# Spare columns between the on-chip tiles of a hybrid decoder layer: operands at 0, 32, 64 and 96 modulo 128 bytes

## The chip, the cores and the metric

The kernel runs on one core of a Trainium2 chip. The metric is the device time of one execution in microseconds. A core has five engines that run side by side: TensorE (PE, with its weight loads shown apart as PEld), VectorE (DVE), ScalarE (ACT), GpSimd (POOL) and SyncE (SP), which issues most of the DMAs. On-chip memory (SBUF) has 128 partitions; a tile lies at one byte offset, the same on every partition. PE sums its products in PSUM.

## The reference

One layer (DEPTH 1) for 512 tokens of width 1024, all in float32:

```python
mod = (cond @ w_ada[l] + b_ada[l])[:, None, :]
sh1, sc1, g1, sh2, sc2, g2 = jnp.split(mod, 6, axis=-1)
h = _rms(x, norm1_w[l]) * (1 + sc1) + sh1
x = x + g1 * _hybrid_mixer(h, w_in[l], ...)
h = _rms(x, norm2_w[l]) * (1 + sc2) + sh2
x = x + g2 * (jnp.square(jax.nn.relu(h @ w_ff1[l])) @ w_ff2[l])
```

`_hybrid_mixer` multiplies h by w_in (1024 x 11,280 columns) and splits the result into the parts of three mixers: a state-space scan (SSD), an attention in three dilated groups, and a pooling over four windows. Each mixer has an output projection and a sigmoid gate; their gated sum goes through w_out.

## The kernel before

**Products in three matmuls.** Every large product runs with operands split into a high and a low part of type float32r (`split`, L310, for activations; `wsplit`, L267, for weights), and `mm3` (L284) issues three matmuls for one block: high weights with low x, high weights with high x, low weights with high x. A matmul has a stationary operand (`lhsT`, 128 columns, loaded before it) and a moving one (`rhs`, 512 columns, 256 where tokens are halved).

`gemm_feat` (L289) has the weights stationary and the activations moving; `gemm_tok` (L301) has the activations stationary (128 tokens of the 512, either next to each other or, with `mod`, every fourth one) and the weights moving. The weights stream in by `wstream` (L274): a DMA of two row blocks, a high part on ScalarE (L270), a low part on VectorE (L271), in three buffers each.

**Names.** hh and hl are the high and low parts of the first normed input, 8 tiles each; gh and gl, in the same places, those of the second. wh and wl are the streamed weights; wsh and wsl those of the first two chunks, Q and K, loaded apart; wrh and wrl weights that are kept (`resident`, L1054). ah and al are the parts of the squared ReLU; yn, pool, mx, o and pd those of the SSD output, the pooling, the gated sum, the attention output and the pooled differences. In the profile a matmul's operands stand as moving, stationary: `psacc<-gl,wh` moves gl over weights wh.

**Order.** The Q and K products of the first chunk (up to some 65 us), and the stretch from the second half of the output projection to the first MLP chunk, are in an order written out by hand; the rest is laid out by the scheduler, with `wstream`'s loads and splits ahead of other work. Pieces of attention, SSD and modulation are handed out between row blocks of weights.

**Where tiles lie.** Pools follow one another in SBUF, and inside a pool each tile follows the one before. cpool holds `cst` (the constants, L159, 328 columns) and then hh0..hh7 and hl0..hl7, 2048 bytes each. sm holds small tiles; raws and wsp the raw and split weights; gp the 59 blocks of 128 x 512 that `Slots` (L116) hands out, the one first that has been free for longest. All other activations and kept weights live in these blocks. In the built program hh and hl start at 32 modulo 128 bytes, all of them; wh, wl and every block of gp start at 96.

Of the kernel before, what the change touches and what calls it, by code (L numbers as in the profile page):

```python
# [28 lines left out]

# [1 line left out]
def _alibi_slopes(n):  # L31
# [53 lines left out]

# columns of the vector table: 128 values each
VCOLS, _at = {}, 0
# [5 lines left out]

# chunks of 512 columns of w_in
Z, XS, BCC, Q, K, VV, U, GS, GA, GP = 0, 2, 4, 5, 8, 11, 14, 16, 18, 20
# [3 lines left out]
def kernel(ctx: ExitStack, tc: tile.TileContext, a: dict, out: bass.AP, dbg=None):  # L99
# [16 lines left out]
    class Slots:  # L116
        """places of [128, 512] float32: the one that has been free for longest goes first"""

        def __init__(self, pool, prefix, n):
            self.pool, self.prefix = pool, prefix  # L120
            self.idle, self.used = list(range(n)), {}

        def take(self, name, dt):
            i = self.idle.pop(0)
            t = self.pool.tile([P, T], dt, tag=f"{self.prefix}{i}", name=uid(name), bufs=1)
            self.used[id(t)] = (i, t)
            return t
# [3 lines left out]

    sb, banks = Slots(gp, "b", NBLK), Slots(pp, "p", 8)

# [22 lines left out]

# [1 line left out]
    ncut = COFF["al0"][0]  # L158
    cst = cpool.tile([P, ncut], F32, name="cst")  # L159

# [21 lines left out]

    # 1/sqrt(sum/n + eps) of a small tile of sums
    def rsqrt_small(ss, n, name):
# [9 lines left out]
    def token_rsqrt(sums, n, name):  # L194
        """1/sqrt(sum over the partitions of sums / n + eps) on every partition, in PSUM"""
        nb = sums.shape[1] // P
        sp = psm(name)
        for b in range(nb):
            mm(sp[:, b : b + 1], lhsT=sums[:, b * P : (b + 1) * P], rhs=ones[:, 0:1], start=True, stop=True)
        ss = small([P, 4], name, 2)[:, :nb]  # L200
        V.tensor_copy(ss, sp[:, :nb])
        free(sp)
        return spread(rsqrt_small(ss, n, name + str(nb)), nb, name)

    def spread(r, nb, name):
        """columns of tokens to rows, the same on every partition, in PSUM"""
        rp = psm(name)
        for b in range(nb):
            dg = small([P, P], "diag", 2)
            V.tensor_scalar(dg, ident, r[:, b : b + 1], None, ALU.mult)  # L210
            mm(rp[:, b * P : (b + 1) * P], lhsT=ones, rhs=dg, start=True, stop=True)
        return rp
# [11 lines left out]

# [1 line left out]
    def ada_load(part, k):  # L226
# [20 lines left out]

    # work beside the large products: handed out one piece per two row blocks of weights
    background = [ada_later(part, k) for part in (2, 3, 4, 5) for k in range(8)]
# [15 lines left out]

# [1 line left out]
    def wsplit(raw, shape):  # L267
# [21 lines left out]
    def gemm_feat(w, nk, ch, ah, al, k0=0):  # L289
        """4 blocks [128 columns of w, 512 tokens]"""  # L290
        ps = [acc() for _ in range(4)]
        for k, wh, wl in wstream(w, nk, ch, k0):
            for j in range(4):
                cs = slice(j * P, (j + 1) * P)
                mm3(ps[j], wh[:, cs], wl[:, cs], ah[k], al[k], k == 0, k == nk - 1)
        return ps
# [4 lines left out]
    def gemm_tok(w, nk, ch, ah, al, mod, ahead=None):  # L301
        """4 blocks [128 tokens, 512 columns of w]; tokens 128 b + p, or 4 p + b with mod"""
        ps = [acc() for _ in range(4)]
# [12 lines left out]
    def evac(ps, name, func=AF.Copy):  # L316
        """out of PSUM, ahead of other work"""
        with tc.high_priority(offset=SOON):
# [10 lines left out]

# [1 line left out]
    E = mybir.EngineType  # L331
    with tc.manual_schedule(engines={E.DVE, E.Activation, E.PE, E.SP}):
# [101 lines left out]
        hh = [cpool.tile([P, T], F32R, name=f"hh{k}", tag=f"hh{k}") for k in range(8)]  # L434
        hl = [cpool.tile([P, T], F32R, name=f"hl{k}", tag=f"hl{k}") for k in range(8)]

# [25 lines left out]
        for k in range(8):  # L462
# [19 lines left out]
            for ch, ps in ((Q, qps), (K, kps)):  # L482
# [3 lines left out]
                free(wh, wl)  # L486
    nc.sync.dma_start(cst[:, P:], a["const"][:, P:ncut])
    free(R1)
# [3 lines left out]

# [1 line left out]
    def take(ps, name):  # L494
        """blocks of q or k out of PSUM, and 1/rms of their heads"""
        xs, ss = evac(ps, name), small([P, 16], "ss" + name, 2)
# [23 lines left out]
    def scores(gi, qs, rq, ks):  # L520
        """pieces of work: transposes of a head, then its scores and exponentials"""
        mx, zs = small([P, 16], f"mx{gi}"), small([P, 16], f"zs{gi}")
# [65 lines left out]
    def exchange(src, mask, sel, name):  # L588
        """[P, 2, (head, i)] -> [P, 2, (head, j)] in the other order of tokens"""
        ps = psm(name)  # L590
# [25 lines left out]
    def joint(stats):  # L616
        """softmax over the three groups: (max, sum) move between the two orders of tokens"""
        (m0, z0), (m1, z1), (m2, z2) = stats
# [20 lines left out]
    def attn_turn(h, probs, fs):  # L639
        """weighted probabilities with keys on partitions"""  # L640
        res = []
# [34 lines left out]

# [1 line left out]
    mixed, mh, ml = [], [], []  # L678
# [25 lines left out]

# [1 line left out]
    v3 = lambda t: t.rearrange("p (c h) -> p c h", h=16)  # L706
    st = {}

    def ssd_steps():
        """step sizes dt [token, (chunk, head)]; p_cum = -a_cum = cumsum(dt exp(a_log)) inside each chunk"""  # L710
        nc.sync.dma_start(hv.rearrange("p a h -> p (a h)"), a["hvec"].broadcast_to([P, 48]))
# [4 lines left out]
        nc.sync.dma_start(wdt, a["w_dt"])  # L716
        # the two parts of the weights side by side
        wd = small([P, 8, 32], "wd", dt=F32R)
# [22 lines left out]
        free(dT, tp)  # L741
        # softplus(x) = max(x, 0) + log1p(e), e = exp(-|x|); log1p(e) = 2 atanh(q), q = e / (2 + e) <= 1/3
        V.tensor_scalar(e, dt, -1.0, None, ALU.mult)
# [27 lines left out]
        yield  # L771
        # rows of p_cum
        tp = psm("pcT")
# [19 lines left out]
    def ssd_states(g, xs, BC):  # L793
        """X = xs dt in token layout, states before each chunk, masked C B^T"""
        BT, CT = BC[g], BC[2 + g]
# [43 lines left out]
    def ssd_heads(g, j, xs, z):  # L839
        """two heads: [128 features, 512 tokens], times silu(z)"""  # L840
        X, prev, cb, CT = st[g]
        pc, npc, prow = st["pc"], st["npc"], st["prow"]
        # p_cum of a head on every partition
        Ms = [blk("M") for _ in range(2)]
# [53 lines left out]

# [1 line left out]
    def pool(half):  # L900
# [36 lines left out]

# [1 line left out]
    yh, yl, dh, dl, ph_, pl_ = [], [], [], [], [], []  # L939
    def pieces(gen):  # L940
        """a generator's steps, as pieces of work"""
        def step():
            next(gen, None)
        return step
# [33 lines left out]
    def do_heads(g, xs, z):  # L978
        # the exponentials of the next two heads stand before the products of these
        gens = [ssd_heads(g, j, xs, z) for j in range(4)]  # L980
# [68 lines left out]

# [1 line left out]
    xT = [blk(f"xr{k}") for k in range(8)]  # L1051
    for k in range(8):
        nc.sync.dma_start(xT[k], a["x"][k])
    def resident(w, ch, k0, n):  # L1054
        """parts of the weights of n row blocks, kept"""
        res = []
# [16 lines left out]
    gh = [cpool.tile([P, T], F32R, name=f"gh{k}", tag=f"hh{k}") for k in range(8)]  # L1073
    gl = [cpool.tile([P, T], F32R, name=f"gl{k}", tag=f"hl{k}") for k in range(8)]
    hw = T // 2
    # the rest of the output projection, the second norm and the first chunk of the MLP, in halves of the tokens:
    # one half's norm runs beside the other half's products
    E = mybir.EngineType
# [100 lines left out]

# [1 line left out]
    def square_relu(ps):  # L1181
# [10 lines left out]
    for half in range(2):  # L1192
# [9 lines left out]
        for ch in range(2):  # L1202
# [5 lines left out]
            else:  # L1208
                # the last rows finish one bank after another, the last bank's tokens in halves
                parts = [(j, full, acc()) for j in range(3)] + [(3, ts, acc()) for ts in halves]  # L1210
# [24 lines left out]
def _laid_out(inputs):  # L1235
    """the inputs in the order in which the kernel reads them"""
    f = {name: np.asarray(inputs[name]) for name in _INS}

    def tiles(w):
        # [K, N] -> [N / 512, K / 256, 128, 2, 512]  # L1240
        k, n = w.shape
        return w.reshape(k // 256, 2, P, n // T, T).transpose(3, 0, 2, 1, 4)
# [32 lines left out]
```

## Time and profile before

| what | value |
|---|---|
| time, median of 3 runs | 1126.01 us (1125.87 to 1126.14) |
| span of the profiled execution | 1123.5 us |
| PE busy | 1116.0 us, 99% of the span, 5414 matmuls |
| weight loads busy | 952.2 us, 85% |
| VectorE busy | 597.9 us, 53% |
| ScalarE busy | 492.2 us, 44% |
| granted TensorE clock | 1.000 |
| DMA | 134.45 MB, mean 120 GB/s |

The profiled execution has no time of its own besides its span; the runs' times hold some 2.5 us more, which lie before the first and after the last instruction of the span. A matmul's record runs from its start to a modelled end and overlaps the next one's, so the time that one matmul takes from the next is read from the starts, or from the count in a stretch.

### The profile page before, as it was taken

To read this page: it belongs to the slowest core of one execution; us is meant where nothing else is said; L and a number is where in the kernel's file an instruction comes from. 1 tells how busy PE (TensorE), PEld (TensorE's weight loads), DVE (VectorE), ACT (ScalarE), POOL (GpSimd) and SP (SyncE) were. 2 spreads that over 40 slices of the span, in tenths; PEclk is the share of its full clock that TensorE was granted. 3 is DMA by queue.
4 is the path that set the end of the run, shared out by engine and by line. 5 is a ranking of instruction groups with operands and counts; after the bars stand their busy time and mean duration, and the time that the engine had idled before them with its cause. 6 is when DMAs were issued, how large, how long until landed. Compare 5 with 4: busy or idle time off the path is not lost.

```text
span 1123.5 us, 14055 instructions
## 1 busy us (share of the span) xinstructions
PE 1116.0 (99%) x5414; PEld 952.2 (85%) x5414; DVE 597.9 (53%) x1210; ACT 492.2 (44%) x937; POOL 0.2 (0%) x4
## 2 busy tenths in 40 slices
PE   8999999999999999999999999999999999999998
PEld 6889998999887888888888888899888888888887
DVE  6973763572667668468833424576354233445241
ACT  5475885543497448425432123353343111344120
POOL 0000000000000000000000000000000000000000
PEclk9999999999999999999999999999999999999999
DMA  9852253333543444322333422360122233322331
GB/s 342 299 183 98 96 164 105 105 104 130 166 135 103 132 142 131 115 83 75 104 113 104 159 94 94 115 204 1 57 93 94 95 101 103 96 95 94 94 131 38
DMA packets 49347, 134.45 MB, mean 120 GB/s; under 512 B 5616, under 2 KB 6384, under 8 KB 49280
## 3 DMA queue, kind: packets, MB, share of 16 engines
q1 hardware_dynamic: 47696, 130.81, 35.6%
q10 hardware_dynamic: 1584, 2.75, 0.8%
q8 instruction: 42, 0.69, 0.2%
q14 instruction: 25, 0.20, 0.1%
HBM read 131.41 MB, written 2.13 MB: 119 GB/s over the span
## 4 chain that ended last, share of the span: by engine, by line
PE 95%; ACT 2%; DVE 2%; DMA 1%; issue 0%; SPq 0%; DVEq 0%; ACTq 0%
PE psacc L285 29%; PE psacc L287 29%; PE psacc L286 29%; PE psS L555 1%; PE psy L867 1%; PE pso L671 1%; PE psyo L875 1%; PE pso L669 1%; DVE conv L786 0%; PE pskT L539 0%; PE psqT L534 0%; PE pspT L652 0%; DVE wa L366 0%; PE psst L827 0%; DMA crow<-in_c_dram 0%; PE pssx L404 0%
## 5 line engine op out<-in xcount | busy, mean ns | idle before, releaser
L271 DVE TENSOR_TENSOR wl<-raw,wh 128x1024 fp32r<-128x1024 f32 x161 | 196.9, 1223 | 348.1 <-ACT wh L270 346.4
L270 ACT CAST wh<-raw 128x1024 fp32r<-128x1024 f32 x161 | 168.9, 1050 | 378.4 <-PE psacc L286 326.2
L285 PE MATMUL psacc<-hl,wh 128*128 128x512 f32 x416 | 168.0, 404 | 0.7 <-ACT prev L830 0.6
L287 PE MATMUL psacc<-hh,wl 128*128 128x512 f32 x416 | 163.2, 392 | 0.0
L286 PE MATMUL psacc<-hh,wh 128*128 128x512 f32 x416 | 162.1, 390 | 0.0
L285 PEld LDWEIGHTS psacc<-hl,wh 128*128 128x128 f32 x416 | 78.3, 188 | 18.0 <-issue 1.2
L287 PEld LDWEIGHTS psacc<-hh,wl 128*128 128x128 f32 x416 | 78.1, 188 | 18.2
L285 PE MATMUL psacc<-wl,hh 128*128 128x512 f32 x224 | 93.4, 419 | 0.0
L286 PEld LDWEIGHTS psacc<-hh,wh 128*128 128x128 f32 x416 | 78.2, 188 | 17.7 <-issue 1.4
L285 PE MATMUL psacc<-al,wh 128*128 128x512 f32 (+1 forms) x242 | 92.1, 381 | 0.0
L286 PE MATMUL psacc<-ah,wh 128*128 128x512 f32 (+1 forms) x242 | 92.1, 381 | 0.0
L287 PE MATMUL psacc<-ah,wl 128*128 128x512 f32 (+1 forms) x242 | 92.1, 380 | 0.0
L286 PE MATMUL psacc<-wh,hh 128*128 128x512 f32 x224 | 90.1, 402 | 0.0
L287 PE MATMUL psacc<-wh,hl 128*128 128x512 f32 x224 | 89.7, 401 | 0.0
L285 PE MATMUL psacc<-gl,wh 128*128 128x512 f32 x224 | 88.3, 394 | 0.0
L287 PE MATMUL psacc<-gh,wl 128*128 128x512 f32 x224 | 87.6, 392 | 0.0
L286 PE MATMUL psacc<-gh,wh 128*128 128x512 f32 x224 | 86.9, 388 | 0.0
L286 PEld LDWEIGHTS psacc<-wh,hh 128*128 128x128 f32 x224 | 65.9, 294 | 1.4
L285 PEld LDWEIGHTS psacc<-wl,hh 128*128 128x128 f32 x224 | 65.5, 293 | 1.7
L287 PEld LDWEIGHTS psacc<-wh,hl 128*128 128x128 f32 x224 | 65.5, 293 | 1.5
L235 DVE SCALAR_TENSOR_TENSOR wa<-wa,crow 128x512 f32<-128x512 f32 x64 | 43.5, 686 | 21.4 <-DMA wa<-in_w_ada_dram 21.3
L285 PEld LDWEIGHTS psacc<-al,wh 128*128 128x128 f32 x242 | 45.5, 188 | 8.9
(342 smaller groups left out, 1914.4 us busy)
## 6 DMA issues: line engine op xcount, KB each, us to landing
raw<-in_w_in_dram SPq DMA_DIRECT2D x80, 512.0 KB, 3.5
raw<-in_w_ff_dram SPq DMA_DIRECT2D x64, 512.0 KB, 3.5
wa<-in_w_ada_dram SPq DMA_DIRECT2D x96, 256.0 KB, 4.6
wst<-in_w_in_dram SPq DMA_DIRECT2D x16, 256.0 KB, 5.4
M<-prow SPq DMA_DIRECT2D x16, 256.0 KB, 3.4
raw<-in_w_ssd_out_dram SPq DMA_DIRECT2D x8, 512.0 KB, 3.5
raw<-in_w_pool_out_dram SPq DMA_DIRECT2D x8, 512.0 KB, 3.4
raw<-in_w_out_dram SPq DMA_DIRECT2D x8, 512.0 KB, 3.4
```

Of the source, the lines that this page charges most:

```text
L235: V.scalar_tensor_tensor(wa[i], wa[i], 1.0, crow[i], ALU.mult, ALU.mult, accum_out=d[:, i : i + 1])
L270: S.copy(wh, raw)
L271: V.tensor_tensor(wl, raw, wh.bitcast(F32), ALU.subtract)
L285: mm(ps, lhsT=wh, rhs=xl, start=first, stop=False)
L286: mm(ps, lhsT=wh, rhs=xh, start=False, stop=False)
L287: mm(ps, lhsT=wl, rhs=xh, start=False, stop=last)
L555: mm(so[b], lhsT=qT[:, b * P : (b + 1) * P], rhs=kT[:, (b + 1) * P - n : (b + 1) * P], start=True, stop=True)
L669: mm(od, lhsT=vs[kb][:, hs], rhs=pT[b // 2][:, cs : cs + P], start=(b == 0), stop=False, skip_group_check=True)
L671: mm(ov[:, b, :], lhsT=vs[b][:, hs], rhs=pT[0][:, b * P : (b + 1) * P], start=False, stop=(gi == 2 and b == 3), skip_group_check=True)
L867: mm(yp[half * 64 : half * 64 + 64, cs], lhsT=X[c][:, (2 * j + half) * 64 : (2 * j + half + 1) * 64], rhs=Ms[half][:, cs], start=True, sto ...
L875: mm(op[:, cs], lhsT=prev[c][:, j * P : (j + 1) * P], rhs=CT[:, cs], start=True, stop=True)
```

## The change

`Slots` gets a number of spare columns; a block of gp is allocated with 8 columns more (2080 bytes in place of 2048) and used without them. hl and gl get 8 spare columns each in the same way. `cst` gets 24 spare columns at its end. The banks of PSUM get none. Comments are left out of the changed file, which leaves the line numbers as they are up to L125; behind it they are one higher.

```diff
     class Slots:
...
-        def __init__(self, pool, prefix, n):
-            self.pool, self.prefix = pool, prefix
+        def __init__(self, pool, prefix, n, gap=0):
+            self.pool, self.prefix, self.gap = pool, prefix, gap
             self.idle, self.used = list(range(n)), {}
 
         def take(self, name, dt):
             i = self.idle.pop(0)
-            t = self.pool.tile([P, T], dt, tag=f"{self.prefix}{i}", name=uid(name), bufs=1)
+            t = self.pool.tile([P, T + self.gap], dt, tag=f"{self.prefix}{i}", name=uid(name), bufs=1)
+            t = t[:, :T]
             self.used[id(t)] = (i, t)
             return t
...
-    sb, banks = Slots(gp, "b", NBLK), Slots(pp, "p", 8)
+    sb, banks = Slots(gp, "b", NBLK, 8), Slots(pp, "p", 8)
...
-    cst = cpool.tile([P, ncut], F32, name="cst")
+    cst = cpool.tile([P, ncut + 24], F32, name="cst")
...
-        hl = [cpool.tile([P, T], F32R, name=f"hl{k}", tag=f"hl{k}") for k in range(8)]
+        hl = [cpool.tile([P, T + 8], F32R, name=f"hl{k}", tag=f"hl{k}")[:, :T] for k in range(8)]
...
-    nc.sync.dma_start(cst[:, P:], a["const"][:, P:ncut])
+    nc.sync.dma_start(cst[:, P:ncut], a["const"][:, P:ncut])
...
-    gl = [cpool.tile([P, T], F32R, name=f"gl{k}", tag=f"hl{k}") for k in range(8)]
+    gl = [cpool.tile([P, T + 8], F32R, name=f"gl{k}", tag=f"hl{k}")[:, :T] for k in range(8)]
```

In the two built programs the instructions of every engine stand in the same order, with the same shapes and names; the addresses differ. The starts of the tiles, modulo 128 bytes:

| tiles | before | after |
|---|---|---|
| hh, gh (8) | 32 | 0 |
| hl, gl (8) | 32 | 0, 32, 64, 96 in turn |
| wh, wl (streamed weights), raw | 96 | 64 |
| the 59 blocks of gp | 96 | 64, 96, 0, 32 in turn |

The large products (4624 float32r matmuls), by the start of the moving operand modulo 128 bytes, counted in the built programs:

| moving operand at | before, 512 columns | after, 512 columns | before, 256 | after, 256 |
|---|---|---|---|---|
| 0 | 0 | 1812 | 0 | 216 |
| 32 | 1936 | 564 | 192 | 128 |
| 64 | 0 | 1215 | 0 | 74 |
| 96 | 2208 | 553 | 288 | 62 |

Of the 4144 with 512 columns, moving and stationary operand lie 0 apart (modulo 128, with the strided weights counted by their tile's start) in 1344 before and 616 after, 64 apart in 2784 and 2314, and 32 or 96 apart in 16 and 1214.

## The prediction

> **What bounds the kernel now.** I read the page's first line, the share of each engine, the chain that ended last, and then the waits of TensorE (PE).
>
> ```profile
> span 1123.5 us, 14055 instructions
> PE 1116.0 (99%) x5414; PEld 952.2 (85%) x5414; DVE 597.9 (53%) x1210; ACT 492.2 (44%) x937; POOL 0.2 (0%) x4
> PE 95%; ACT 2%; DVE 2%; DMA 1%; issue 0%; SPq 0%; DVEq 0%; ACTq 0%
> PE psacc L285 29%; PE psacc L287 29%; PE psacc L286 29%; PE psS L555 1%; PE psy L867 1%; PE pso L671 1%; PE psyo L875 1%; PE pso L669 1%; DVE conv L786 0%; PE pskT L539 0%; PE psqT L534 0%; PE pspT L652 0%; DVE wa L366 0%; PE psst L827 0%; DMA crow<-in_c_dram 0%; PE pssx L404 0%
> ```
>
> The reader is to see that three lines, the three matmuls of `mm3`, hold 87% of the chain, and that PE stands in it for 95%. The longest wait that PE has for any engine is short:
>
> ```profile
> PE pssx L404 <- DVE sq L403: 1.6, 1, 1.6
> ```
>
> So the time is the number of matmuls times their pace. The page's mean of one matmul (389 to 419 ns) is a length with the pipeline in it; the pace is the distance from start to start. I take it from stretches in which PE does large products alone (columns: stretch; its length, then PE, weight loads, VectorE, ScalarE and GpSimd, each busy us and count; PE clock; DMA share; GB/s):
>
> ```profile
> 32.00:64.00 32.00, 32.00 (x138) 25.77 (x138) 31.58 (x86) 17.29 (x30) 0.00 (x0) 1.00 0.85 292
> 164.00:192.00 28.00, 28.00 (x120) 25.77 (x120) 12.34 (x28) 18.76 (x65) 0.00 (x0) 1.00 0.37 113
> 306.00:334.00 28.00, 28.00 (x124) 22.99 (x123) 19.45 (x37) 24.24 (x34) 0.00 (x0) 1.00 0.44 137
> 745.00:755.00 10.00, 10.00 (x86) 10.00 (x85) 8.71 (x14) 4.21 (x8) 0.00 (x0) 1.00 0.57 183
> 860.00:944.00 84.00, 84.00 (x372) 69.56 (x372) 25.22 (x27) 16.80 (x17) 0.00 (x0) 1.00 0.31 100
> 946.00:1031.00 85.00, 85.00 (x373) 69.76 (x372) 34.53 (x40) 29.48 (x40) 0.00 (x0) 1.00 0.30 96
> ```
>
> A record of 0.39 us that begins every 0.23 us reaches over a border, so a window counts 1.7 matmuls too many (2.4 for the short ones of the fourth row). The paces, with the places of the operands modulo 128 bytes (moving / stationary): 860 to 944 us, second MLP product, 96/96: 84.00 / 370.3 = 226.8 ns. 946 to 1031, first MLP product, 32/96: 85.00 / 371.3 = 228.9. 306 to 334, the same form with hh and hl, 32/96: 228.9. 32 to 64, the Q and K products, 96/32: 234.8. 164 to 192, the same with every fourth token as weights: 236.7. The 256-column matmuls at 745, 96/96: 10.00 / 83.6 = 119.6. The clock is 1.00 in all of them. The first MLP product differs from the second by nothing on PE but the tile that moves, 32 against 96, so the place can matter, by 2.1 ns at least. Nor are other engines the reason: VectorE is busy for 99% of the first stretch and 30% of the fifth, DMA for 0.85 and 0.31, and within a stretch the starts repeat to 0.01 us:
>
> ```profile
> 990.38 0.39 PE L285 MATMUL psacc<-gl,wh 128*128 128x512 f32 x1
> 990.62 0.39 PE L286 MATMUL psacc<-gh,wh 128*128 128x512 f32 x1
> 990.84 0.39 PE L287 MATMUL psacc<-gh,wl 128*128 128x512 f32 x1
> 991.07 0.39 PE L285 MATMUL psacc<-gl,wh 128*128 128x512 f32 x1
> ```
>
> What is there to win: 256 more columns cost 226.8 - 119.6 = 107.2 ns, so one costs 0.419 ns, 512 cost 214.4, and 12.4 ns of each large matmul is a fixed part.
>
> **The change, part by part.** No instruction is added, removed or moved: the order on every engine is the same, and so are the DMAs, the bytes and the shapes. Only addresses differ. (1) 24 spare columns in `cst` put hh and gh at 0 in place of 32. (2) Eight spare columns after each hl and gl put them at 0, 32, 64, 96 in turn. (3) The same after each of the 59 blocks does it for the parts of a, yn, pool, mx and o and for the kept weights. (4) The streamed weights wh and wl shift from 96 to 64 behind them. Nothing is queued behind a new wait. VectorE, ScalarE and the DMAs get other addresses; I cost that at nothing, because PE hides it: in the page's shares above they are busy for 53% and 44% of the span. That cover is thin only from 20 to 65 us, where VectorE is the second engine at its limit (31.58 of 32.00 us), so a faster PE wins nothing there and I leave those 192 matmuls out.
>
> The new pairs of places stand in no stretch of this trace, so their price is a bound from both sides. From below: the fixed part goes where the moving operand starts at 0 or 64. That is so for 3027 of 4144 matmuls of 512 columns (of them 96 before 65 us) and 290 of 480 of 256; 2931 x 12.4 + 290 x 12.4 = 40 us won. From above: every product takes the worst unit-stride pace, 234.8. That is 1344 x 8.0 for those at 226.8 and 1920 x 5.9 for those at 228.9: 22 us lost. Between them I take this: both places of before, 32 and 96, start in the middle of a 64-byte piece, and 2048 bytes that start so touch 33 pieces, in place of 32. One piece is 16 columns, 16 x 0.419 = 6.7 ns, a little over half of the fixed part, which is nearest to what the rows can hold (two pieces would be 13.4, more than all of it). That memory is read in such pieces no row shows; the 6.7 ns are an estimate from the rows at 745 and 860. The sum:
>
> - 512 columns, moving operand at 0 or 64, after 65 us: 2931 x 6.7 = 19.6 us
> - 256 columns: 290 x 6.7 = 1.9 us
> - less half of the gain of the 576 products with strided weights, all of them among the 2931: 576 x 6.7 / 2 = 1.9 us. Their loads are the long ones:
>
> ```profile
> L286 PEld LDWEIGHTS psacc<-wh,hh 128*128 128x128 f32 x224 | 65.9, 294 | 1.4
> L286 PEld LDWEIGHTS psacc<-hh,wh 128*128 128x128 f32 x416 | 78.2, 188 | 17.7 <-issue 1.4
> ```
>
> A load of 294 ns in a pace of 236.7 may itself hold that pace; I can't tell, and take half.
>
> Together 19.6 us, so the span would go from 1123.5 to 1103.9. The median of the runs, 1126.01, lies 2.5 us over the span, for what is outside it; that stays. 1126.0 - 19.6 = 1106.
>
> [...]
>
> **The rivals.**
>
> *Slower: the operands fall out of step.* The fastest pace, 226.8, is the one where both operands stand at the same place; 64 apart it is 228.9 one way round and 234.8 the other. If the two streams that PE reads side by side disturb each other by their distance, then hh against the streamed weights stays as it was (64 apart before and after), while the 1344 products that were in step are scattered over four distances. Of all 4144 matmuls of 512 columns, 1344 had distance 0 before and 616 have it after, and 1214 stand at 32 or 96 apart, which the trace doesn't show. Price: three quarters of the 1344, 1000, go from 226.8 to something from 228.9 to 234.8, 2.1 to 8.0 us; a third of the 1920 products of h and g, those with hl or gl, lose 0 to 5.9 ns each, 0 to 3.8 us. Together 2 to 12 us; I put it at 1131. It decides if the distances of 32 and 96 cost more than the start at 0 or 64 saves. For it: Q and K, with the same moving place 96 as the second MLP product, are 8.0 ns slower, and what differs is the place of the weights. Against it: first MLP product and Q, K have the same distance and differ by 5.9.
>
> [...]
>
> *Only a start at 0 counts (pieces of 128 bytes).* Then 1764 matmuls of 512 columns after 65 us (1812 less 48) and 216 of 256 lose the whole fixed part: 1980 x 12.4 = 25 us, 1101. For it: 226.8 and 119.6 lie nearly 32 columns over 214.4 and 107.2. Against it: the two pieces of 64 would be more than the whole fixed part, with nothing left for the change of weights.
>
> *The place does nothing, or gains and losses cancel.* Then the paces differ because x and w change roles, and it is 1126. Against it is the pair of MLP products, which differ in the place alone.
>
> **How the numbers follow.** Pieces of 64 bytes 0.36 (1106, with its own range 1100 to 1116); pieces of 128 bytes 0.18 (1101); a small gain where both effects meet 0.04 (about 1120); nothing 0.10 (1126); out of step 0.32 (1131). The range reaches over the cases to 1097 and 1134; the 2 in 10 left out are the whole fixed part won (1086) and the worst pace for all (1148). By 0.2% (2.3 us, about what a measurement of this kernel can tell from no change): faster 0.58, same 0.11, slower 0.31.
>
> **What would show it.** Counts and order stay; the paces move. Right: the first MLP product, whose gh starts at 0, goes from 228.9 to about 222; the second, a mixture, to about 223; hh and hl likewise; the strided products to 230 to 236. Out of step: the second MLP product goes above 227 and loses its even starts, and the first hardly moves. If all strides keep their paces to 0.5 ns, the place does nothing. Wrong in another way would be a new wait of PE for VectorE or a DMA of more than the 1.6 us above, or a longer mean of the weight loads' 188 ns.

## The result, and the profile after

The changed kernel takes 1134.12 us (median of 4 runs, 1133.64 to 1134.61) against 1126.08 us before (4 runs): 8.0 us more, a ratio of 1.0071 with a 95% interval of 1.0057 to 1.0084. It is slower, where 1106 us was forecast.

The page's first line, PE's share and the chain by engine are as before but for the time:

```profile
span 1132.8 us, 14055 instructions
PE 1124.5 (99%) x5414; PEld 951.0 (84%) x5414; DVE 599.0 (53%) x1210; ACT 491.7 (43%) x937; POOL 0.2 (0%) x4
PE 95%; ACT 2%; DVE 2%; DMA 1%; issue 0%; SPq 0%; DVEq 0%; ACTq 0%
```

The same number of matmuls, the same 95% of the chain on PE, so the pace must have changed. The same stretches of the program as in the prediction, in the changed kernel (stretch; its length, then PE, weight loads, VectorE, ScalarE and GpSimd, busy us and count; PE clock; DMA share; GB/s):

```profile
34.00:65.00 31.00, 31.00 (x136) 25.10 (x135) 30.59 (x82) 16.41 (x27) 0.00 (x0) 1.00 0.77 266
165.00:192.00 27.00, 27.00 (x117) 25.01 (x117) 11.66 (x27) 20.11 (x70) 0.00 (x0) 1.00 0.37 114
307.00:335.00 28.00, 28.00 (x123) 22.81 (x122) 19.48 (x38) 24.85 (x33) 0.00 (x0) 1.00 0.44 134
746.00:756.00 10.00, 10.00 (x79) 9.64 (x78) 8.61 (x13) 5.57 (x9) 0.00 (x0) 1.00 0.50 176
864.00:951.00 87.00, 87.00 (x376) 70.36 (x375) 26.15 (x26) 17.98 (x20) 0.00 (x0) 1.00 0.29 96
953.00:1040.00 87.00, 87.00 (x379) 70.87 (x378) 35.79 (x42) 30.25 (x42) 0.00 (x0) 1.00 0.30 97
```

With the 1.7 matmuls that a window counts too many taken off, the second MLP product goes at 87.00 / 374.3 = 232.4 ns (226.8 before) and the first at 87.00 / 377.3 = 230.6 (228.9 before). The fourth row can't be read against its like: it holds products of 512 columns beside those of 256. The even beat of the second MLP product is gone. Before, all its steps were 0.226 or 0.227 us, as in these lines of PE's timeline:

```profile
900.16 0.39 PE L285 MATMUL psacc<-al,wh 128*128 128x512 f32 x1
900.39 0.39 PE L286 MATMUL psacc<-ah,wh 128*128 128x512 f32 x1
900.62 0.39 PE L287 MATMUL psacc<-ah,wl 128*128 128x512 f32 x1
900.84 0.39 PE L285 MATMUL psacc<-al,wh 128*128 128x512 f32 x1
```

After, the steps lie anywhere from 0.224 to 0.238 us:

```profile
900.14 0.39 PE L286 MATMUL psacc<-al,wh 128*128 128x512 f32 x1
900.37 0.39 PE L287 MATMUL psacc<-ah,wh 128*128 128x512 f32 x1
900.61 0.40 PE L288 MATMUL psacc<-ah,wl 128*128 128x512 f32 x1
900.84 0.40 PE L286 MATMUL psacc<-al,wh 128*128 128x512 f32 x1
```

Taken from all starts of the trace (the mean step from one start to the next, steps of over 300 ns left out), the paces and what they make of the time are:

| products | matmuls | before, ns | after, ns | us |
|---|---|---|---|---|
| a, 512 columns | 720 | 227.2 | 232.0 | +3.5 |
| yn, pool, mx, o, pd, 512 columns | 624 | 227.4 | 232.1 | +2.9 |
| h and g, 512 columns | 1920 | 229.2, 228.9 | 231.0, 230.7 | +3.5 |
| weights moving over every fourth token of h | 576 | 238.1 | 236.4 | -1.0 |
| weights moving over neighbouring tokens of h (V) | 96 | 233.4 | 232.6 | -0.1 |
| 256 columns | 480 | 119.0 to 120.7 | 118.0 to 119.8 | -0.3 |

Together 8.5 us, against 8.0 measured; the 192 Q and K products before 65 us, which the table leaves out, go from 233.3 to 231.6 ns and take 0.3 us off again. (The spans differ by 9.3 us, since this profile also has a slower start: a granted clock of 0.92 over its first 22 us in place of 1.00, and a wait of PE of 2.8 us in place of 1.6. The profile of the first experiment's kernel has that start too, with 0.92 and 2.6 us, at an unchanged median; it isn't the change's.)

### The profile page after: what moved, and what is told of

Same layout as the page of the kernel before. It is cut to its first block, busy times and chain, and to the rows that moved or that the text cites. A ratio compares the mean times of both kernels' runs of the same rounds, so it can differ in the third digit from the quotient of the medians.

```text
span 1132.8 us, 14055 instructions
## 1 busy us (share of the span) xinstructions
PE 1124.5 (99%) x5414; PEld 951.0 (84%) x5414; DVE 599.0 (53%) x1210; ACT 491.7 (43%) x937; POOL 0.2 (0%) x4
## 4 chain that ended last, share of the span: by engine, by line
PE 95%; ACT 2%; DVE 2%; DMA 1%; issue 0%; SPq 0%; DVEq 0%; ACTq 0%
PE psacc L286 29%; PE psacc L288 29%; PE psacc L287 29%; PE psS L556 1%; PE psy L868 1%; PE pso L672 1%; PE psyo L876 1%; PE pso L670 1%; PE pssx L405 1%; DVE conv L787 0%; PE pskT L540 0%; PE psqT L535 0%; PE pspT L653 0%; DMA crow<-in_c_dram 0%; DVE wa L367 0%; PE psst L828 0%
## 5 line engine op out<-in xcount | busy, mean ns | idle before, releaser
L287 PEld LDWEIGHTS psacc<-ah,wh 128*128 128x128 f32 x242 | 45.4, 188 | 10.0
```

Source lines behind the costliest of these rows:

```text
L287: mm(ps, lhsT=wh, rhs=xh, start=False, stop=False)
```

## The experiments

Three theories are at stake: *pieces* (the prediction: a moving operand that starts at 0 or 64 modulo 128 is cheaper); *distance* (what counts is how far apart PE's two operands lie, modulo some number of bytes; the prediction's slower rival); and *rhythm* (a fast beat needs the same places from one matmul to the next). Each experiment starts from the kernel before.

**All operands moved by 32 bytes.** This keeps every distance and puts every operand at 0 or 64 modulo 128.

```diff
-    cst = cpool.tile([P, ncut], F32, name="cst")
+    cst = cpool.tile([P, ncut + 8], F32, name="cst")
```

(The DMA that fills `cst` is fitted to it, as in the change.)

> Eight spare columns (32 bytes) behind the constants alone move every operand of the large products by 32 bytes: hh, hl, gh, gl from 32 to 64, the streamed weights and the blocks from 96 to 0 (modulo 128 bytes). All distances stay as they were before. Pieces of 64 bytes (the prediction): every moving operand now starts at a multiple of 64, 6.7 ns less in some 3950 matmuls of 512 columns and 480 of 256, so some 28 us less, 1098 us. Distance or rhythm theory (only where the operands lie against one another counts): paces of 226.8 (second MLP product) and 228.9 ns (first) stay to 0.5 ns, 1126 us within 2 us.

1125.71 us against 1125.78, a ratio of 1.0001 (0.9992 to 1.0010). The two MLP products (stretches of the windows view):

```profile
862.00:945.00 83.00, 83.00 (x368) 68.75 (x367) 24.27 (x25) 16.39 (x16) 0.00 (x0) 1.00 0.31 99
948.00:1032.00 84.00, 84.00 (x369) 68.98 (x368) 34.08 (x40) 28.94 (x40) 0.00 (x0) 1.00 0.29 95
```

83.00 / 366.3 = 226.6 ns and 84.00 / 367.3 = 228.7: as before. The pieces are refuted; a start at 0 or 64 in place of 32 or 96, taken by itself, wins nothing here.

**The blocks' gaps alone.**

```diff
-            t = self.pool.tile([P, T], dt, tag=f"{self.prefix}{i}", name=uid(name), bufs=1)
+            t = self.pool.tile([P, T + (8 if self.prefix == "b" else 0)], dt, tag=f"{self.prefix}{i}", name=uid(name), bufs=1)[:, :T]
```

> Of the change only the eight spare columns behind each of the 59 blocks; constants, hh, hl and the streamed weights lie as before. Distance or rhythm theory: the products of a, yn, pool, mx and o lose their common place with the weights and go from 226.8 to about 232 ns as in the changed kernel, 1344 x 5.4 = 7 us; h and g stay at 228.9; about 1133 us. Pieces of 64 bytes: half of these 1344 start at 0 or 64 and gain 6.7 ns, 4.5 us less, 1121 us.

1132.34 us, ratio 1.0053 (1.0036 to 1.0070), 6.6 us more. The second and the first MLP product:

```profile
862.00:950.00 88.00, 88.00 (x380) 71.21 (x379) 27.11 (x28) 19.49 (x22) 0.00 (x0) 1.00 0.28 93
952.00:1038.00 86.00, 86.00 (x378) 70.62 (x376) 35.41 (x42) 29.77 (x42) 0.00 (x0) 1.00 0.29 95
```

88.00 / 378.3 = 232.6 ns and 86.00 / 376.3 = 228.5. By all starts a goes at 232.0 ns, yn, pool, mx, o and pd at 232.3, while h and g keep 229.1 and 228.9. This half of the change holds most of the loss.

**The gaps of hl and gl and the shift of `cst` alone.**

```diff
-    cst = cpool.tile([P, ncut], F32, name="cst")
+    cst = cpool.tile([P, ncut + 24], F32, name="cst")
...
-        hl = [cpool.tile([P, T], F32R, name=f"hl{k}", tag=f"hl{k}") for k in range(8)]
+        hl = [cpool.tile([P, T + 8], F32R, name=f"hl{k}", tag=f"hl{k}")[:, :T] for k in range(8)]
```

(gl likewise, and the DMA of `cst`.)

> Of the change only the 24 spare columns behind the constants and the eight behind each hl and gl; the blocks have no gaps and all lie at 64, with the streamed weights. Distance or rhythm theory: a, yn, pool, mx and o keep 226.8 ns; h and g go from 228.9 to 230.7 as in the changed kernel (1920 x 1.7 = 3.3 us), the strided products from 238 to 236 (576 x 2 = 1.2 us less); about 1128 us. Pieces of 64 bytes: all products of a and of the hh, gh halves gain 6.7 ns; 1105 us or less.

1127.83 us, ratio 1.0019 (1.0009 to 1.0028), 2.1 us more. The second and the first MLP product:

```profile
864.00:946.00 82.00, 82.00 (x364) 67.93 (x363) 23.91 (x24) 16.23 (x16) 0.00 (x0) 1.00 0.30 97
950.00:1034.00 84.00, 84.00 (x366) 68.47 (x365) 35.00 (x41) 30.44 (x42) 0.00 (x0) 1.00 0.29 97
```

82.00 / 362.3 = 226.3 ns and 84.00 / 364.3 = 230.6. By all starts h and g go at 231.0 and 230.7 ns, the strided products (those over every fourth token) at 236.5, a unchanged at 227.1. The two halves, 6.6 and 2.1, add up to the change's 8.0 within their spread.

**One common place.** 80 spare columns behind the last hl put the streamed weights and the blocks at the same place as hh and hl, modulo 512 bytes.

```diff
-        hl = [cpool.tile([P, T], F32R, name=f"hl{k}", tag=f"hl{k}") for k in range(8)]
+        hl = [cpool.tile([P, T + (80 if k == 7 else 0)], F32R, name=f"hl{k}", tag=f"hl{k}")[:, :T] for k in range(8)]
```

(gl likewise.)

> 80 spare columns (320 bytes) behind the last hl alone: the streamed weights and the blocks move from 96 to 32 modulo 128, and to the same place as hh and hl modulo 512 bytes. No other gap. Distance theory: the products of h and g go from 228.9 to 226.8 ns (1920 x 2.1 = 4.0 us) and the Q, K and V products with unit stride from 234 to 227 (those after 65 us: 96 x 7 = 0.7 us), the strided ones from 238 to between 227 and 238 (0 to 6 us): 1115 to 1122 us. Pieces of 64 bytes: every operand still starts at 32, nothing changes, 1126 us. If the paces depend on something other than distances, they stay as they were or go either way.

1119.77 us, ratio 0.9946 (0.9931 to 0.9961): 6.0 us faster than before. The second and first MLP product, a stretch of strided products that passes into V at 180.6 us, and the products of hh and hl, in this order:

```profile
856.00:938.00 82.00, 82.00 (x363) 67.94 (x363) 24.07 (x24) 17.07 (x18) 0.00 (x0) 1.00 0.29 97
942.00:1025.00 83.00, 83.00 (x368) 68.78 (x367) 34.77 (x40) 28.83 (x39) 0.00 (x0) 1.00 0.29 96
165.00:191.00 26.00, 26.00 (x113) 24.20 (x113) 10.75 (x25) 17.81 (x60) 0.00 (x0) 1.00 0.36 111
306.00:333.00 27.00, 27.00 (x120) 22.36 (x120) 18.86 (x37) 24.61 (x33) 0.00 (x0) 1.00 0.43 137
```

83.00 / 366.3 = 226.6 ns for the first MLP product (228.9 before) and 27.00 / 118.3 = 228.2 for hh and hl. From all starts: g 226.7, h 227.4, the V products 227.6 in place of 233.4, the strided ones 235.3 in place of 238.1. The distance decides here, in the products of both forms. (The products of g with 256 columns get slower by it, 121.1 ns in place of 119.1.)

**The scan of distances.** A kernel without the layer runs 72 large matmuls for each of 32 cases. `wt` and `mv` lie at the same place modulo 2048; d is the distance in bytes from the weights to the moving operand, dl how much further its low part lies.

```python
at = d // 4
xh, xl = mv[:, at : at + T], mv[:, 4 * T + at + dl // 4 : 5 * T + at + dl // 4]
...
nc.tensor.matmul(ps, lhsT=wh, rhs=xl, start=r == 0, stop=False)
nc.tensor.matmul(ps, lhsT=wh, rhs=xh, start=False, stop=False)
nc.tensor.matmul(ps, lhsT=wl, rhs=xh, start=False, stop=r == count - 1)
```

> Leaves out the whole layer: 32 cases of 72 large matmuls each (512 columns, in the order of the kernel's three matmuls) from two tiles that lie at the same place modulo 2048 bytes, with the moving operand put d bytes behind the weights; d from 0 to 480 in steps of 32, 1024, 4 and 16; four cases in which the low part lies 32, 64, 128 or 256 bytes further than the high one; eight cases with every fourth column as weights. Its output is not the layer's. A matmul's mean length minus 162 ns is its pace. Distance theory: the paces of the kernel come back at the same distances: 226.8 at 0, 228.9 at 320, 233.4 at 192, 238 at 192 and 235 at 0 with strided weights, and other distances lie between 225 and 240. If the pace depended on what else runs in the kernel, the paces would be equal here at all distances. Pieces of 64 bytes: steps of 32 bytes alternate by 6.7 ns.

Four cases by the view of a tile (line, engine, operation, tile, count; length in ns, least, median and most; first and last start in us), d of 0, 64, 128 and 192. The first matmul of a group of three is shown, so that 69 matmuls lie between the two starts:

```profile
L165 PE MATMUL psab<-mv,wt x24: 389/389/390, 28.3 to 44.0; 128*128 128x512 f32 x24
L165 PE MATMUL psad<-mv,wt x24: 388/388/397, 61.5 to 77.3; 128*128 128x512 f32 x24
L165 PE MATMUL psaf<-mv,wt x24: 392/394/399, 94.8 to 110.9; 128*128 128x512 f32 x24
L165 PE MATMUL psah<-mv,wt x24: 394/394/400, 128.4 to 144.5; 128*128 128x512 f32 x24
```

15.7 / 69, 15.8 / 69 and twice 16.1 / 69: 227.5, 229.0, 233.3 and 233.3 ns, each within 1.5. From the starts in ns, the mean of the last 40 steps of each case:

| d, bytes | 0 | 32 | 64 | 96 | 128 | 160 | 192 | 224 |
|---|---|---|---|---|---|---|---|---|
| pace, ns | 226.7 | 233.4 | 228.9 | 233.5 | 233.3 | 234.3 | 233.3 | 233.4 |
| pace at d + 256 | 226.7 | 233.3 | 228.9 | 233.5 | 233.3 | 234.3 | 233.4 | 233.4 |
| every fourth column as weights | 235.0 | | 240.0 | | 240.0 | | 238.4 | |

Over the 512 bytes scanned the pace repeats after 256: the first two rows agree to 0.1 ns at all eight distances. (Each case writes the next of eight PSUM tiles in turn, so d and d + 256 in the first two rows share their tile as well. The tile isn't the cause: with every fourth column as weights d and d + 256 write different tiles, and their paces agree to 0.1 ns at all four distances.) The scan has the kernel's paces with nothing else running: 228.9 for h and g before (64 from the weights), 233.3 for Q, K and V (192), 238.4 for the strided ones (192). Its rows also price the change: blocks in steps of 2080 bytes take all eight distances in turn, and the mean of the first row is 232.1, where the changed kernel has 232.0 and 232.1; since mixing can add to a mean, as the next paragraph shows, so close an agreement is partly luck. Steps of 32 bytes don't alternate as the pieces would have it (32, 96, 160 and 224 are slow, but so are 128 and 192).

Rhythm counts besides. With the low part 32, 64 or 128 bytes further and the high part at distance 0 (one matmul of three at the other distance) the paces are 231.6, 231.8 and 233.3; for 64, a mean of the single paces would be (2 x 226.7 + 228.9) / 3 = 227.4. Mixing the two best places of the table costs more than either of them. With the low part 256 bytes further it is 226.7 again.

**The same place modulo 128 and 256 alone; modulo 2048.** The same edit with 16 and with 464 columns behind the last hl in place of 80.

> As the kernel with hh, hl and the weights at the same place, but with 16 spare columns (64 bytes): the same place modulo 128 and 256, 256 bytes apart modulo 512. If the distance counts modulo 128 or 256, it is as there: h and g at 226.8 ns, about 1120 us. If it counts modulo 512 or more, h and g take another pace, between 226 and 235, 1118 to 1135 us.

> As the kernel with hh, hl and the weights at the same place, but with 464 spare columns (1856 bytes): the same place modulo 2048, in place of modulo 512 alone. If the distance counts modulo 512 or less, all paces are as there, 1120 us within 2; if it counts modulo 1024 or 2048, h, g and the strided products take other paces.

1119.29 us, ratio 0.9939 (0.9922 to 0.9955), and 1119.73 us, 0.9942 (0.9927 to 0.9956). All paces are those of the common place modulo 512, to 0.5 ns. More than 256 bytes of agreement win nothing. The kernel with 16 spare columns is the fastest of all, 6.7 us under the kernel before and, by the medians of two sets of runs, 14.8 under the changed one; the three kernels with one common place can't be told apart.

**Gaps of 128 bytes.** This keeps all places modulo 128, but not modulo 256.

```diff
-            t = self.pool.tile([P, T], dt, tag=f"{self.prefix}{i}", name=uid(name), bufs=1)
+            t = self.pool.tile([P, T + (32 * (i % 2) if self.prefix == "b" else 0)], dt, tag=f"{self.prefix}{i}", name=uid(name), bufs=1)[:, :T]
```

> 32 spare columns (128 bytes) behind every second of the 59 blocks: all places modulo 128 as before, but the blocks of a, yn, pool, mx and o lie 0, 128, 256 or 384 from the weights modulo 512, and so from one another. Distance modulo 128: the second MLP product stays at 226.8 ns, 1126 us. Distance modulo 512: it goes to about 232 as with the gaps of 32 bytes, 1132 us.

1128.70 us, ratio 1.0022 (1.0013 to 1.0032). The second MLP product (first row) is slower, the first (second row) is not:

```profile
862.00:946.00 84.00, 84.00 (x367) 68.54 (x366) 23.98 (x25) 16.39 (x16) 0.00 (x0) 1.00 0.28 100
950.00:1034.00 84.00, 84.00 (x369) 68.95 (x368) 34.81 (x41) 30.27 (x42) 0.00 (x0) 1.00 0.29 100
```

84.00 / 365.3 = 230.0 ns, and the scan's mean of distances 0 and 128 is (226.7 + 233.3) / 2 = 230.0. The expectation with a modulus of 512 had 232, with 128 it had 226.8; both missed. The places modulo 128, in which the change is described, are not what counts.

**Narrow weights.** The scan again, with weights of 64 and 32 columns, 256 moving columns, and distances that are no multiples of 32 (one of its three matmul lines; the others likewise).

```diff
-            nc.tensor.matmul(ps, lhsT=wh, rhs=xl, start=r == 0, stop=False)
+            nc.tensor.matmul(ps[:cols, :m], lhsT=wh, rhs=xl, start=r == 0, stop=False)
```

> As the scan of distances (the layer is left out, the output is not the layer's), with weights of 128, 64 and 32 columns, with a moving operand of 256 columns, and with distances that are no multiples of 32. If the fixed part of a matmul comes from the load of the next weights, which is read beside the moving operand, it shrinks with the columns: 128 columns 226.7 ns at distance 0 and 233.3 at 128, 64 columns about half of the parts over 214.4 (220 and 224), 32 columns a quarter. If it comes from the change between matmuls, it stays for 32 columns. 256 columns: 119.6 at distance 0, 118 at 64. Distances 240, 248, 252 and 8: between 231 and 237, as 16 and 4 were.

| d, bytes | 0 | 64 | 128 | 192 |
|---|---|---|---|---|
| 128 columns of weights | 226.7 | 228.8 | 232.2 | 233.3 |
| 64 columns | 229.9 | 228.4 | 229.4 | 232.7 |
| 32 columns | 231.7 | 231.7 | 230.7 | 231.7 |
| 128 columns, 256 columns moving | 120.0 | 117.8 | 118.7 | 113.3 |

Two cases of 32 columns, at d of 0 and 128, in the view of the tile:

```profile
L156 PE MATMUL psaj<-mv,wt x24: 389/392/397, 160.5 to 176.5; 128*32 128x512 f32 x24
L156 PE MATMUL psal<-mv,wt x24: 387/396/401, 193.9 to 209.8; 128*32 128x512 f32 x24
```

16.0 / 69 = 231.9 and 15.9 / 69 = 230.4. The first side of the expectation missed: the shorter load doesn't shrink the pace here, and with a quarter of the columns to load (records of 109 ns in place of 188) it lies 16 to 17 ns over the prediction's 214.4. By the other side that excess would stay as it is; at distance 0 it grows by 5.0 ns. But the distance matters less with the shorter loads: with 32 columns the four paces lie within 1.0 ns, with 64 within 4.3, with 128 within 6.6. At 128 the first scan had 233.3 where this one has 232.2, with another order of steps, so this pace comes back to about a nanosecond only. At distances of 240, 248, 252 and 8 the paces are 236.7, 230.0, 226.7 and 233.4 (the first scan had 236.7 at 4 and 231.7 at 16); 252 misses its expected 231 to 237, and so does 248, by 1.0. Lying 4 bytes behind the weights' place cost 10.0 ns in these scans, lying 4 bytes before it nothing. The two paces expected for 256 moving columns came, but there the best distance is 192, not 0.

**Gaps that keep the place.** The change's idea with gaps of 256 bytes, behind each hl and gl and behind every fourth block, and 16 columns more behind the last hl.

```diff
-            t = self.pool.tile([P, T], dt, tag=f"{self.prefix}{i}", name=uid(name), bufs=1)
+            t = self.pool.tile([P, T + (64 if self.prefix == "b" and i % 4 == 0 else 0)], dt, tag=f"{self.prefix}{i}", name=uid(name), bufs=1)[:, :T]
...
-        hl = [cpool.tile([P, T], F32R, name=f"hl{k}", tag=f"hl{k}") for k in range(8)]
+        hl = [cpool.tile([P, T + (80 if k == 7 else 64)], F32R, name=f"hl{k}", tag=f"hl{k}")[:, :T] for k in range(8)]
```

(gl likewise.)

> Gaps again, but of 64 spare columns (256 bytes): behind each hl and gl and behind every fourth of the 59 blocks, with 16 more columns behind the last hl, so that all operands keep the same place modulo 256. If the distance modulo 256 is the cause, gaps as such do nothing and the time is that of the kernels with one common place, 1119.5 us within 1.5; if unequal tile distances as such break the rhythm, it is above 1123.

1119.87 us, ratio 0.9950 (0.9933 to 0.9966), as the kernels with one place and no gaps. The second and the first MLP product:

```profile
856.00:938.00 82.00, 82.00 (x363) 67.93 (x362) 23.29 (x23) 16.44 (x16) 0.00 (x0) 1.00 0.30 98
942.00:1025.00 83.00, 83.00 (x368) 68.76 (x367) 33.86 (x39) 29.30 (x40) 0.00 (x0) 1.00 0.30 97
```

82.00 / 361.3 = 227.0 and 83.00 / 366.3 = 226.6 ns. Gaps that keep the place cost nothing here; the distances that the change's gaps make cost 8.0 us.

## Why the prediction was wrong

**What bounds the kernel** was right: the whole difference is the pace of the large matmuls, with the same order and the same engines beside them. That the pace doesn't hang on other engines was right too: the scan has the kernel's paces, 228.9 ns at distance 64 and 233.3 at 192, with no other work beside it.

**The step that failed** is the price of the new places: "both places of before, 32 and 96, start in the middle of a 64-byte piece", 6.7 ns for each operand moved to 0 or 64. The pieces were the author's assumption, which no row showed. The term was worth 19.6 us and measured nothing (1125.71 against 1125.78 with all operands so placed). Its rows had all been taken at one alignment, 32 modulo 64, and a number of the size of the fixed part was read as a cause. Nor is the fixed part of 12.4 ns one number: worked out in the same way from the narrow scan (twice the pace of 256 columns less that of 512) it is 13.3 at distance 0, 6.8 at 64, 5.2 at 128 and -6.7 at 192. A fixed part can't be less than nothing, so these two lengths don't split the pace into columns and a rest. The term of half the gain for strided loads falls with it.

**The rival that ended on the other side**, operands out of step at 1131 us, was the mechanism, and the time lies at the upper end of the range, 0.1 us beyond its 1134.0. It was sized by a modulus of 128, and that misread two things. "Three quarters of the 1344" keep no place: over the eight places modulo 256 about seven eighths leave it (whether the eighth that stays keeps its pace no run tells apart); the loss was 4.8 ns over all 1344, 6.4 us, in the range of 2.1 to 8.0 given. The 0 to 3.8 us for hl and gl measured 3.5 us, but 1.8 ns over all 1920, those with hh and gh too, because the mixed places break the beat of the neighbours: the steps that begin with gh over wh, whose distance stays, go from 226.3 to 229.9 ns, and those with gl over wh, whose distances scatter, from 231.7 to 231.9. That the sum of 2 to 12 us holds the 8.0 is therefore partly luck: it had too few products, and 1.0 us that the strided ones gain is not in it. And the argument against it, that the first MLP product and Q, K "have the same distance and differ by 5.9", was the period at work: 64 and 192 are one distance modulo 128 and two modulo 256, 228.9 and 233.3 ns.

Two of the rows were also misread in size. By their starts the Q and K products from 32 to 64 us go at 233.3 ns, not 234.8 (one matmul more or less in a window of 138 is 1.7 ns), so the 5.9 is 4.4 and the 8.0 is 6.6. The stretch from 164 to 192 holds V's products with unit stride from 180.7 us on, so its 236.7 is a mean of 238 and 233.

**A term put at nothing** was the 192 products before 65 us, where VectorE is at its limit and "a faster PE wins nothing". The kernel with 16 spare columns says otherwise:

```profile
34.00:64.00 30.00, 30.00 (x134) 24.87 (x133) 29.59 (x81) 16.62 (x29) 0.00 (x0) 1.00 0.82 286
```

VectorE is as busy, at 29.59 of 30.00 us, and PE goes at 30.00 / 132.3 = 226.8 ns. From the start of the first to that of the last of the 192 it takes 45.0 us in place of 46.0, so 1.0 of the 6.7 us is won there.

**The other rivals.** Pieces of 128 bytes fall with the first experiment, where the second MLP product started at 0 throughout at 226.6 ns. "The place does nothing" falls with the common place, 1119.77 us against 1125.78. The scan has 226.7 to 234.3 ns among starts that are all multiples of 32 bytes; with the moving operand's length and the loads equal, the distance alone makes 7.6 ns. Whether the reading of the moving operand or that of the next weights is held up no run here shows.

**Its signs of the rival** held: "the second MLP product goes above 227 and loses its even starts" came; "the first hardly moves" was 1.7 ns.

Open is why. In the trace of before the next weights are loaded while an operand moves: the load from 990.39 to 990.58 us lies within the matmul from 990.38 to 990.78. That such a load disturbs the matmul by distance would agree with the loads of 32 columns, where the four distances differ by 1.0 ns alone; but those matmuls are no faster at distance 0 (231.7 ns against 226.7), so the columns of the load are not the whole cause. No run here shows what the period of 256 bytes is a property of, nor why matmuls of 256 columns have their best distance elsewhere (113.3 ns at 192, 120.0 at 0).

## What to carry to other kernels

Where matmuls of one length go at several paces with no engine waiting, compare the addresses of the two operands, modulo powers of two, before looking for a start that is cheap in itself; a uniform shift of all tiles and a shift of one pool against the others tell the two apart, at a line of code each (here 1125.71 and 1119.77 us, against 1125.78). Here, with float32r products of 512 columns over 128 columns of weights, keeping moving operand, weights and the tiles of neighbouring matmuls at the same place modulo 256 bytes is worth 0.6% (1119.29 us against 1126.01), and 16 spare columns in one tile reach it. For other shapes measure the distances first: with 256 columns the best of four was 192, at 113.3 ns. Spreading tiles over places was no remedy here: a mixture ran at the mean of the paces (230.0 ns over distances 0 and 128), or above it (231.8 against 227.4).

## What the hardware showed that was not expected

- In the scan of distances the pace of float32r matmuls of 512 columns and 128 columns of weights went by the distance of the operands modulo 256 bytes: 226.7 ns at 0, 228.9 at 64, 233.3 to 234.3 at 32, 96, 128, 160, 192 and 224; between these steps it is 236.7 at 4 and 226.7 at 252. Moving all operands by 32 bytes together did nothing (1125.71 against 1125.78 us).
- One matmul at distance 64 to two at 0 gave 231.8 ns, above the paces of both distances (226.7 and 228.9) and above their mean, 227.4.
- With 256 moving columns the order was another one: 113.3 ns at 192, 117.8 at 64, 118.7 at 128, 120.0 at 0.
- With 32 columns of weights the pace was 230.7 to 231.7 ns at the four distances tried: 5.0 slower than with 128 columns at distance 0, 2.9 slower at 64, and 1.5 and 1.6 faster at 128 and 192.
- The pace of 512 columns less that of 256 was 106.7 ns at distance 0 and 120.0 at 192, so a cost per column read from these two lengths holds for the one distance.
